# A hand-written order of units, whole-tile splits and step-free turns in the feed-forward nets of a two-layer fp32 block

## The chip, the cores and the metric

The kernel runs on one core of one Trainium2 chip. The metric is device time in microseconds (us) of the whole program, the median of several runs. Profiles are one traced execution each; times inside a trace count from the first instruction.

## The reference, cut to what matters

One sequence of 256 tokens of width 1024 goes through two layers. Each layer is a feed-forward net (FFN), a token mixer, a cross attention to 256 memory rows, and a second FFN, each followed by a layer norm:

```python
for l in range(DEPTH):                                   # DEPTH = 2
    h = layer_norm(ALPHA * h + 0.5 * swiglu(h, ffn1_gate[l], ffn1_up[l], ffn1_down[l]), ...)
    z = h @ w_in[l]                                      # mixer: short conv, linear recurrence, pooling
    ...
    h = layer_norm(ALPHA * h + mix @ w_out[l], ...)
    h = layer_norm(ALPHA * h + cross_attn(h, mem, ca_q[l], ca_k[l], ca_v[l], ca_o[l]), ...)
    h = layer_norm(ALPHA * h + 0.5 * swiglu(h, ffn2_gate[l], ffn2_up[l], ffn2_down[l]), ...)

def swiglu(x, w_gate, w_up, w_down):                     # 1024 -> 2816 -> 1024
    return (silu(x @ w_gate) * (x @ w_up)) @ w_down
```

## The kernel before, in words

**Precision.** Every fp32 operand of a product is split into a high part (`hi`, rounded by a copy on ScalarE, ACT) and the rest (`lo`, a subtraction on VectorE, DVE). `split` (L60 to L62) is this pair: L61 on ACT, then L62 on DVE, which reads what L61 wrote. A product is three matmuls (`mm_rows`, L130): hi*hi, hi*lo, lo*hi. L106 is the line of nearly every matmul.

**Weights.** `load` (L64) brings weights from device memory in pieces of 1 MB (a `raw` tile of 128 x 2048, three of them in a ring, fetched on the SyncE queue, SP) and splits each piece in two halves of 128 x 1024 into `whi` and `wlo` tiles, eight of each. A half's tiles come free when its last matmul is done.

**FFN.** 2816 hidden columns go in five chunks of 512 and one of 256. Of a chunk there are two pieces of the gate weights, two of the up weights and two of the down weights. `hidden` (L488) computes gate and up for both halves of the tokens (i = 0, 1), `activate` and `gated` (L405, L408) evict them, `turn` (L415) brings the result to hidden-by-token form: four DMAs (`dealt<-sg`) and two 32x32-block transposes on DVE (L422), whose input and output both run in steps, then a split. Rows of the down weights are fetched strewn (`strewn`, L79: partition p takes rows 4p to 4p+3), which is the order that the stepped turn leaves. `both` (L556) adds a down piece into four PSUM tiles. Chunks are interleaved: gate and up of chunk c, then the second half of down of c-2, then the first half of c-1. The last three down pieces are the tail: `finish` (L292) runs them once for each of the four (token half i, column half n) and evicts each with the layer norm's steps L320 (residual), L322 (statistics), L324, L326, L327 (on GpSimd, POOL), L330 and L334.

**Token-major to width-major.** The next stage needs the normed `h` transposed (`xT`). For token half 0 this is done by eight TensorE (PE) transposes (L170, `transposed`) inside the last part of the tail. For token half 1 the function that `finish` returns, `pend`, is called by the next stage between its products; the first chunk of an FFN (`first`, L428) computes i = 0 of gate, half of up, then calls `pend`, then goes on. After `ffn1`, whose follower is the mixer, token half 0 takes another way: `deal` (L532) copies `h` on ACT in steps, sends it through four DMAs, and `dealt` transposes it on DVE (L546) and splits it with stepped writes after the norm of half 1. Keys of the attention (`keys`, L599) run between `ffn1` and the mixer, and there `pend` stands before the fourth of four column products.

**Order.** The instruction order of each engine is made by a scheduler from priorities (order of the program text) and modelled times; it puts another ready instruction between two that depend on each other. `tc.manual_schedule(engines=...)` keeps the instructions of a block in their written order on the engines named, while instructions from outside the block may still come between. Before the change only the start of the first FFN (PE, ACT, DVE), the mixer (PE) and the recurrence's end (DVE) are written by hand.

Of the kernel before, what the change touches and what calls it, by code (L numbers as in the profile page):

```python
# [8 lines left out]
F32 = mybir.dt.float32  # L9
# [5 lines left out]
E = mybir.EngineType  # L15
# [16 lines left out]
PAD = 16  # L32


class Weights:
# [5 lines left out]
    def at(self, k, cols):  # L41
        j, kk = divmod(k, self.per)
        return self.hi[j][:, kk, cols], self.lo[j][:, kk, cols]


@with_exitstack
def model(ctx: ExitStack, tc: tile.TileContext, t: dict, out: bass.AP):
# [16 lines left out]
    def load(src, k0, nk, c0, ncol, fine=False, strewn=False):  # L64

        hi, lo, todo = [], [], []
        step = 2048 // ncol
        for a in range(k0, k0 + nk, step):  # L70
            raw = wp.tile([P, 2048], F32, tag="raw", name="raw", bufs=3)
            raw = raw.rearrange("p (k c) -> p k c", c=ncol)
            half = step // 2
            part = 1 if fine else step
            for b in range(0, step, part):
                loads.append(nc.sync.dma_start(
                    raw[:, b : b + part, :],
                    src[:, c0 : c0 + ncol].rearrange("(p k) c -> p k c", p=P)[:, a + b : a + b + part, :]
                    if strewn  # L79
                    else src[(a + b) * P : (a + b + part) * P, c0 : c0 + ncol].rearrange("(k p) c -> p k c", p=P),  # L80
                ))
            for s in range(2):
                h = wp.tile([P, 1024], F32R, tag="whi", name="whi", bufs=8)
                w = wp.tile([P, 1024], F32R, tag="wlo", name="wlo", bufs=8)
                h = h.rearrange("p (k c) -> p k c", c=ncol)
                w = w.rearrange("p (k c) -> p k c", c=ncol)
                r = raw[:, s * half : (s + 1) * half, :]
                if fine:
                    todo += [(h[:, b, :], w[:, b, :], r[:, b, :]) for b in range(half)]
                else:  # L90
                    split(h, w, r)
                hi.append(h)
                lo.append(w)
        return Weights(hi, lo, half, todo)
# [29 lines left out]
    def add(dst, o):  # L124
        dst = dst if len(dst.shape) == 3 else halves(dst)
# [27 lines left out]

    jdn = cst.tile([P, P], F32, name="jdn")
# [12 lines left out]
    def transposed_half(src, i, j, dh, dl, unit=idn):  # L167
# [3 lines left out]
        split(dh[:, 4 * j : 4 * j + 4, tok(i)], dl[:, 4 * j : 4 * j + 4, tok(i)], pt)  # L171

    def transposed(src, i, dh, dl, unit=idn):
        for j in range(2):
            transposed_half(src, i, j, dh, dl, unit)
# [28 lines left out]
    rows = cst.tile([P, P], F32, name="rows")  # L204
# [10 lines left out]
    def small_parameters(op):  # L215
        nc.gpsimd.memset(rows, 0.0)
# [68 lines left out]
    def ln_params(l, n):  # L285
        g = wp.tile([P, DM], F32, tag="lng", name="lng")
        b = wp.tile([P, DM], F32, tag="lnb", name="lnb")
        nc.sync.dma_start(g, t["ln_g"][l, n : n + 1, :].to_broadcast([P, DM]))
        nc.sync.dma_start(b, t["ln_b"][l, n : n + 1, :].to_broadcast([P, DM]))
        return g, b  # L290

    def finish(mm, y, scale, gb, last=False, flip=False, deal=None):  # L292
# [6 lines left out]
        for i in range(NT):  # L299
# [8 lines left out]
            for c in pieces:  # L308
# [37 lines left out]
    def project_back(slabs, late, gb, scale, between=lambda: None):  # L346
# [30 lines left out]
        return finish(tail, y, scale, gb)  # L377
# [681 lines left out]
```

## Time and profile before

| | |
|---|---|
| device time, 3 runs | 1097.89, 1098.06, 1099.81 us; median 1098.06 us |
| span of the profiled execution, first to last instruction | 1094.9 us; no device time is given for this execution by itself, the runs above lie 3.0 to 4.9 us over its span |
| granted PE clock | 0.998 |
| PE busy | 1079.6 us (99%), 6035 matmuls |
| DVE busy | 836.3 us (76%), of this 468.8 us in 388 `wlo` splits of 128x1024 |
| ACT busy | 585.0 us (53%), of this 398.0 us in 388 `whi` casts of 128x1024 |
| device memory read | 216.15 MB |

In the rows of the trace a line has the start, the time of the merged group, the engine, the source line, the operation, the tiles (written<-read), the shape and a count; what stands in brackets is idle time of that engine before it and what ended it.

### The profile page before, as it was taken

The numbers are of one execution on the slowest core, as the hardware profiler recorded it, in microseconds if no ns is written. First come the engines' busy times: TensorE is split into PE (matmuls) and PEld (weight loads), VectorE is DVE, ScalarE is ACT, GpSimd is POOL, SyncE is SP. The second block draws the span as 40 slices with busy tenths as digits, with TensorE's granted clock in tenths as the row PEclk, the third lists the DMA queues.
The fourth block names the chain that finished last, engine by engine and source line by source line (L and its number), as shares of the span: only waits on it lengthen the run. The fifth ranks groups of instructions, "written<-read, shape, count | busy, mean of one in ns | idle before, by whom it ended". The sixth has DMA issues, their size and how long they took to land.

```text
span 1094.9 us, 15563 instructions
## 1 busy us (share of the span) xinstructions
PE 1079.6 (99%) x6035; PEld 952.6 (87%) x6035; DVE 836.3 (76%) x1075; ACT 585.0 (53%) x811; POOL 61.0 (6%) x113
## 2 busy tenths in 40 slices
PE   9999999999999999999999999999999999999997
PEld 7888888889898888888888888888898988888886
DVE  6679678898889877666687655798988888766665
ACT  6456454767556455444455445457774644544450
POOL 9500001000000000000000000010000000000000
PEclk9999999999999999999999999999999999999999
DMA  9986665754575486766488666647536664876641
GB/s 326 302 285 226 212 215 170 244 180 164 185 273 176 141 293 217 237 214 217 154 266 265 218 216 206 231 143 261 183 135 217 229 208 163 259 242 211 219 167 38
DMA packets 123818, 232.90 MB, mean 213 GB/s; under 512 B 6432, under 2 KB 46656, under 8 KB 118624
## 3 DMA queue, kind: packets, MB, share of 16 engines
q1 hardware_dynamic: 121952, 229.53, 62.9%
q0 software_dynamic: 1216, 1.20, 0.4%
q8 instruction: 47, 0.77, 0.3%
q10 hardware_dynamic: 576, 1.18, 0.3%
q14 instruction: 27, 0.22, 0.1%
HBM read 216.15 MB, written 1.05 MB: 198 GB/s over the span
## 4 chain that ended last, share of the span: by engine, by line
PE 90%; DVE 7%; ACT 2%; issue 1%; DMA 0%; DVEq 0%; ACTq 0%
PE acc L106 60%; PE dn L106 27%; DVE wlo L62 2%; PE acc L170 1%; DVE square L971 1%; PE dn L766 1%; ACT xT L61 0%; DVE qTl L62 0%; DVE h L334 0%; ACT whi L61 0%; DMA h<-in_x_dram 0%; DVE h L330 0%; PE dn L825 0%; DVE xT L62 0%; DVE st L322 0%
## 5 line engine op out<-in xcount | busy, mean ns | idle before, releaser
L62 DVE TENSOR_TENSOR wlo<-raw,whi 128x1024 fp32r<-128x1024 f32 (+1 forms) x396 | 474.1, 1213 | 181.4 <-ACT whi L61 170.6
L61 ACT CAST whi<-raw 128x1024 fp32r<-128x1024 f32 (+1 forms) x396 | 402.5, 1040 | 312.4 <-PE dn L106 117.3
L106 PE MATMUL acc<-whi,xT 128*128 128x512 f32 x1312 | 395.0, 380 | 0.0
L106 PEld LDWEIGHTS acc<-whi,xT 128*128 128x128 f32 x1312 | 247.8, 189 | 35.2
L106 PE MATMUL acc<-wlo,xT 128*128 128x512 f32 x656 | 248.6, 379 | 0.0
L106 PE MATMUL acc<-xT,whi 128*128 128x512 f32 x576 | 142.6, 382 | 4.0 <-DVE xT L62 4.0
L106 PEld LDWEIGHTS acc<-wlo,xT 128*128 128x128 f32 x656 | 124.0, 189 | 17.5
L106 PE MATMUL dn<-whi,ah 128*128 128x512 f32 x346 | 131.3, 379 | 0.0
L106 PE MATMUL dn<-wlo,ah 128*128 128x512 f32 x346 | 131.1, 379 | 0.0
L106 PE MATMUL dn<-whi,al 128*128 128x512 f32 x346 | 131.1, 379 | 0.0
L106 PEld LDWEIGHTS acc<-xT,whi 128*128 128x128 f32 x576 | 103.8, 190 | 16.3 <-ACT whi L61 4.6
L106 PE MATMUL dn<-whi,xT 128*128 128x512 f32 x288 | 88.8, 383 | 0.0
L106 PEld LDWEIGHTS acc<-xT,wlo 128*128 128x128 f32 x576 | 75.6, 191 | 4.3 <-DVE wlo L62 0.4
L106 PE MATMUL acc<-xT,wlo 128*128 128x256 f32 x576 | 76.4, 275 | 0.0
L106 PEld LDWEIGHTS dn<-wlo,ah 128*128 128x128 f32 x346 | 65.4, 189 | 9.3
L106 PEld LDWEIGHTS dn<-whi,al 128*128 128x128 f32 x346 | 65.4, 189 | 9.3
L106 PEld LDWEIGHTS dn<-whi,ah 128*128 128x128 f32 x346 | 65.4, 189 | 9.2
L422 DVE STREAM_TRANSPOSE square<-dealt 128x512 f32<-128x512 f32 x40 | 63.8, 1658 | 0.8 <-DMA dealt<-sg 0.7
L327 POOL TENSOR_TENSOR rs<-rs,nhalf 128x1 f32<-128x1 f32 x16 | 14.9, 929 | 867.3 <-DVE rs L326 859.8
L106 PEld LDWEIGHTS dn<-whi,xT 128*128 128x128 f32 x288 | 54.4, 190 | 8.5 <-DVE xT L62 1.1
L106 PE MATMUL dn<-wlo,xT 128*128 128x512 f32 x144 | 54.7, 380 | 0.0
L320 DVE SCALAR_TENSOR_TENSOR h<-h,dn 128x512 f32<-128x512 f32 x31 | 21.2, 684 | 31.4 <-PE dn L106 31.4
(206 smaller groups left out, 980.3 us busy)
## 6 DMA issues: line engine op xcount, KB each, us to landing
raw<-in_ffn_up_dram SPq DMA_DIRECT2D x44, 1024.0 KB, 4.9
raw<-in_ffn_down_dram SPq DMA_DIRECT2D x44, 1024.0 KB, 5.1
raw<-in_ffn_gate_dram SPq DMA_DIRECT2D x42, 1024.0 KB, 5.0
raw<-in_w_in_dram SPq DMA_DIRECT2D x24, 1024.0 KB, 4.9
dealt<-sg SPq DMA_DIRECT2D x88, 128.0 KB, 3.2
raw<-in_ca_k_dram SPq DMA_DIRECT2D x8, 1024.0 KB, 5.0
raw<-in_w_out_dram SPq DMA_DIRECT2D x8, 1024.0 KB, 4.7
raw<-in_ca_v_dram SPq DMA_DIRECT2D x8, 1024.0 KB, 4.9
```

What stands on the lines that cost most here:

```text
L61: nc.scalar.copy(hi, src)
L62: lows.append(nc.vector.tensor_tensor(lo, src, hi.bitcast(F32), op=ALU.subtract))
L106: nc.tensor.matmul(o, w, x, start=start, stop=stop)
L170: nc.tensor.transpose(pt[:, k, :], src[:, (4 * j + k) * P : (4 * j + k + 1) * P], unit)
L320: nc.vector.scalar_tensor_tensor(v, v, ALPHA / scale, sums(y[i][n]), op0=ALU.mult, op1=ALU.add)
L327: nc.gpsimd.tensor_tensor(rs, rs, nhalf[:, 0:1], op=ALU.pow)
L422: nc.vector.transpose(d.rearrange("p k (i b) -> p b k i", b=4), x[:, :, i, :].rearrange("p b (j k) -> p b k j", k=4))
L766: nc.tensor.matmul(o[g, hh, :], kc[:, hh, g], x, start=True, stop=True)
L971: nc.vector.transpose(pt.rearrange("p m (i r b) -> p b (m i) r", i=2, b=4), pr[hh])
```

## The change

1. `split_tiles`: four `whi` and four `wlo` tiles of 128x2048 in place of eight of 128x1024. In the FFNs a piece is split by one ACT cast and one DVE subtraction of 128x2048. `load`, which serves the other stages and the first chunk of the program, still splits in halves, but both halves lie in one tile, which comes free as a whole.
2. The FFNs are lists of units of 12 matmuls (`plain_chunk`, `down_chunk`; `half_chunk` for the last 256 columns). `run_units` writes them, and `pump` queues, after the unit that uses a piece last, the split of the next piece; at the start it queues four. Everything in it is kept in this order on PE, DVE and ACT. The order of the products is the one of before, by four rows of k for each token half in place of two.
3. The turn: the deal's DMAs are queued at once, the transposes and splits two units later (`defer`). The transposes read and write without steps (`(b r)`, `(k j)`). For that the tokens of `xT` stand in another order inside an FFN (identity `pdn` with permuted columns in the transposes), and down rows are fetched in four DMAs of 32 partitions for each piece (`down_piece`). In the last, narrow chunk the evictions write in steps to undo the token order.
4. `deal` of the mixer's tokens is gone: after `ffn1` token half 0 is transposed on PE within the tail as elsewhere.
5. Smaller: `ah`, `al` have two buffers in place of three and `sg` two in place of one, except in the first FFN; `lng`, `lnb` are one tile `gb`; `rows` lies in another pool. `BLOCKS` is empty, so the functions for block products (`block_chunk`, `forms`, `blocked`) are there but produce no instruction.

The diff, cut to its core:

```diff
+    RAW = 3
+    WIDE = 4
+    def split_tiles(ncol):
+        h = wp.tile([P, 2048], F32R, tag="whi", name="whi", bufs=WIDE)
+        w = wp.tile([P, 2048], F32R, tag="wlo", name="wlo", bufs=WIDE)
 ...
     def load(src, k0, nk, c0, ncol, fine=False):
-            for s in range(2):
-                h = wp.tile([P, 1024], F32R, tag="whi", name="whi", bufs=8)
-                w = wp.tile([P, 1024], F32R, tag="wlo", name="wlo", bufs=8)
 ...
+            h, w = split_tiles(ncol)
+                for b in range(0, step, step // 2):
+                    split(*(x[:, b : b + step // 2, :] for x in (h, w, raw)))
 ...
+    pdn = cst.tile([P, P], F32, name="pdn")
+    nc.vector.tensor_copy(
+        pdn.rearrange("p (r b) -> p r b", b=4), idn.rearrange("p (b r) -> p r b", b=4)
+    )
 ...
-    def finish(mm, y, scale, gb, last=False, flip=False, deal=None):
+    def finish(mm, y, scale, gb, last=False, units=(idn, idn)):
-                        None if last or not i or not n or deal else lambda: transposed(h[0], 0, xTh, xTl),
+                        None if last or not i or not n else lambda: transposed(h[0], 0, xTh, xTl, units[0]),
-            if deal and not i:
-                dealt = deal(h[0])
-        if deal:
-            dealt()
-        return lambda: transposed(h[1], 1, xTh, xTl, jdn if flip else idn)
+        return lambda: transposed(h[1], 1, xTh, xTl, units[1])
 ...
+            def turn(c, x):
+                ah, al = act_tiles()
+                for i in range(NT):
+                    d = fp.tile([P, 4, P], F32, tag="up", name="square")
+                    nc.vector.transpose(
+                        d.rearrange("p k (b r) -> p b k r", b=4), x[:, :, i, :].rearrange("p b (k j) -> p b k j", j=32)
+                    )
+                    split(ah[:, :, tok(i)], al[:, :, tok(i)], d)
-                        d.rearrange("p k (i b) -> p b k i", b=4), x[:, :, i, :].rearrange("p b (j k) -> p b k j", k=4)
 ...
+                def prepare():                                  # of piece(...)
+                    p.hi, p.lo = split_tiles(p.ncol)
+                        split(p.hi, p.lo, p.raw)
 ...
+            def down_piece(c, u):
+                        src = down[c * CHUNK : (c + 1) * CHUNK].rearrange("(a k j) c -> a j k c", a=4, j=32)
+                        for a in range(4):
+                            loads.append(nc.sync.dma_start(
+                                raw[a * 32 : a * 32 + 32], src[a, :, 2 * u : 2 * u + 2, :]
+                            ))
 ...
+                        if a == 1 and kind == "gate":           # a unit of plain_chunk, after its 12 matmuls
+                            activate(state["s"], i, o)
+                        if a == 1 and kind == "up":
+                            gated(state["s"], i, o)
+                            if i == 1:
+                                x = deal(state["s"])
+                                defer(lambda: turn(c, x), 2)
 ...
+                            add(                                # half_chunk
+                                (s if kind == "gate" else r)[:, j, :].rearrange("p (i b r) -> p i r b", i=NT, b=4),
+                                mm_cols(w, slice(j * P, (j + 1) * P), xT).rearrange("p x h (r b) -> p x h r b", b=4),
+                            )
 ...
+                def pump(free):                                 # run_units
+                    live -= free
+                    while True:
+                        while fetched < len(order) and (raws < RAW if order[fetched].ring else order[fetched].free()):
+                            order[fetched].fetch()
+                            raws += order[fetched].ring
+                            fetched += 1
+                        if made == len(order) or live == WIDE:
+                            return
+                        order[made].prepare()
+                        raws -= order[made].ring
+                        live += 1
+                        made += 1
+
+                pump(0)
+                for x, (ws, run) in enumerate(units):
+                    for f in [f for at, f in waiting if at <= now[0]]:
+                        f()
+                    run()
+                    now[0] += 1
+                    pump(sum(final[w] == x for w in ws))
 ...
+                if pend is not None:                            # sequence
+                    seq += [g[0][0], g[1][0], u[0][0], call(pend), u[1][0], g[0][1], g[1][1], u[0][1], u[1][1]]
+                for c in range(1, end_chunk):
+                    for x in (*g, *u):
+                        seq += x
+                    if c > 1:
+                        seq += downs[c - 2][1]
+                    seq += downs[c - 1][0]
 ...
+            end = [down_piece(end_chunk - 1, 0), down_piece(end_chunk - 1, 1), down_piece(end_chunk, 0)]
+            with tc.manual_schedule(engines=ffn_engines):       # PE, DVE, ACT
+                run_units(sequence(), end)
```

More of the change, by code (lines that the diff above doesn't have):

```diff
@@ L584, in ffn @@
-            end = [slab(4, 0), slab(4, 1), slab(5, 0)]
-            def tail(i, m, cols, alone, between):
-                for u, a in enumerate(end):
-                    if between is not None and u == 1:
-                        between()
-                    for k in range(2):
-                        first = alone is not None and u == 0 and k == 0
-                        rows_of(a, i, k, m, first, u == 2 and k == 1, cols, alone)
-            mixer_next = name == "ffn1"
-            return finish(tail, ys, 0.5, gb, last=last, flip=mixer_next, deal=deal if mixer_next else None)
+                ah, al = act_rows(c, i, 2 * u + k)
@@ L599, in keys @@
+            return finish(tail, ys, 0.5, held["gb"], last=last, units=(idn, jdn) if name == "ffn1" else (pdn, pdn))
     def keys(l, c, between={}):
@@ L1030, in model @@
         pend = attention(l, pend)
[L1031 removed]
+        pend = ffn(l, "ffn2", 3, pend, last=l == DEPTH - 1, blocks=BLOCKS[2 * l + 1])
 _INS = [
```

549 lines of the change are left out of this document (368 added, 181 removed).

## The prediction

> **What bounds the kernel now.** I read the page's busy times first, then its slices, then stretches of the FFNs, then the few waits of TensorE (PE).
>
> ```profile
> span 1094.9 us, 15563 instructions
> PE 1079.6 (99%) x6035; PEld 952.6 (87%) x6035; DVE 836.3 (76%) x1075; ACT 585.0 (53%) x811; POOL 61.0 (6%) x113
> PE   9999999999999999999999999999999999999997
> ```
>
> PE is busy for all but 15.3 us. A busy PE can still be waiting a little between pipelined matmuls, so the spacing inside the FFNs decides (windows: time, then busy time and count for PE, PEld, DVE, ACT, POOL, clock, DMA share, GB/s; the sum is over 384 to 520, 557 to 690 and 925 to 1056).
>
> ```profile
> 384.00:520.00 136.00, 136.00 (x636) 119.20 (x635) 93.92 (x88) 67.79 (x77) 0.00 (x0) 1.00 0.72 235
> sum 400.00, PE 400.00 PEld 350.40 DVE 273.12 ACT 198.25 POOL 0.00; mean PE 133.33 PEld 116.80 DVE 91.04 ACT 66.08 POOL 0.00
> ```
>
> 636 matmuls in 136 us are 214 ns each, without a gap: a unit of 12 takes 2.57 us, a piece (24) 5.13 us. DVE has 127 us free of 400 there, ACT 202. So inside an FFN there is nothing to win: what DVE and ACT save there lies beside a full PE. The change computes the same products, so it can win or lose only where PE waits now, or where it will.
>
> **The change part by part.**
>
> **The deal after ffn1 goes.** Waits (count, longest), then the timeline of layer 0 and one set of eight transposes elsewhere:
>
> ```profile
> PE acc L106 <- DVE xT L62: 4.0, 2, 2.0
> ...
> 186.84 1.30 DVE L546 STREAM_TRANSPOSE square<-dealt 128x512 f32<-128x512 f32 x2
> 188.73 2.13 DVE L62 TENSOR_TENSOR xT<-square,xT 128x512 fp32r<-128x512 f32 x2 [0.29 <-ACT xT L61]
> 193.68 1.75 PE L106 MATMUL acc<-xT,whi 128*128 128x512 f32 x7 [2.02 <-DVE xT L62]
> ...
> 371.59 1.04 PE L170 MATMUL acc<-idn,h 128*128 128x128 f32 x8
> 372.38 0.46 PE L106 MATMUL dn<-whi,xT 128*128 128x512 f32 x1
> ```
>
> These two waits, 2.0 us in each layer, are where the mixer's first product waits for the second token half, whose split stood on DVE behind 3.4 us of the deal's transposes and stepped splits (1.30 + 2.13). They go, and with them two ACT copies, four DMAs on SP and the stepped casts. In their place the splits of token half 0 (1.28 us for a pair, quoted below) stand earlier, in the tail, and eight transposes on PE, which cost it 372.38 - 371.59 = 0.79 us. DVE is 2.1 us lighter before the wait, so I take the 2.02 as gone; what is late next is the `lo` half of w_in, needed 1.7 us later. Net 2.02 - 0.79 = 1.23 us won, twice: -2.5. Ends: -2.5 (wait gone whole) and +1.6 (wait stays, transposes added).
>
> **Wide splits where a stage begins with `pend`.** This happens three times: attention to ffn2 in both layers, ffn2 to ffn1 between them. The first, ACT, then DVE, then PE:
>
> ```profile
> 371.19 2.00 ACT L61 CAST whi<-raw 128x1024 fp32r<-128x1024 f32 x2 [12.02 <-PE dn L106]
> 373.10 1.05 ACT L61 CAST xT<-acc 128x512 fp32r<-128x512 f32 x2
> 374.05 3.88 ACT L61 CAST whi<-raw 128x1024 fp32r<-128x1024 f32 x4
> ...
> 372.35 2.34 DVE L62 TENSOR_TENSOR wlo<-raw,whi 128x1024 fp32r<-128x1024 f32 x2
> 374.61 1.28 DVE L62 TENSOR_TENSOR xT<-acc,xT 128x512 fp32r<-128x512 f32 x2
> 375.81 0.68 DVE L320 SCALAR_TENSOR_TENSOR h<-h,dn 128x512 f32<-128x512 f32 x1
> 376.40 1.22 DVE L62 TENSOR_TENSOR wlo<-raw,whi 128x1024 fp32r<-128x1024 f32 x1
> 377.54 0.69 DVE L322 BATCH_NORM_STATS2 st<-h 128x6 f32<-128x512 f32 x1
> 378.14 1.21 DVE L62 TENSOR_TENSOR wlo<-raw,whi 128x1024 fp32r<-128x1024 f32 x1
> 379.26 0.20 DVE L324 BATCH_NORM_AGGREGATE mv<-st 128x2 f32<-128x12 f32 x1
> 379.38 1.17 DVE L62 TENSOR_TENSOR wlo<-raw,whi 128x1024 fp32r<-128x1024 f32 x1
> 380.53 1.41 DVE L330 SCALAR_TENSOR_TENSOR h<-h,mv,lng 128x512 f32<-128x512 f32 x2
> 381.86 1.41 DVE L334 SCALAR_TENSOR_TENSOR h<-h,rs,lnb 128x512 f32<-128x512 f32 x2
> 383.18 1.22 DVE L62 TENSOR_TENSOR wlo<-raw,whi 128x1024 fp32r<-128x1024 f32 x1
> 384.31 1.29 DVE L62 TENSOR_TENSOR xT<-acc,xT 128x512 fp32r<-128x512 f32 x2
> ...
> 375.49 0.59 PE L106 MATMUL acc<-whi,xT 128*128 128x512 f32 x2
> 382.82 1.22 PE L170 MATMUL acc<-idn,h 128*128 128x128 f32 x8
> ```
>
> Here DVE has no gap from 372.35 to 385.6, and PE is fed with no slack: the `xT` subtraction of token half 0 has its first result near 375.3, the matmul that reads it starts at 375.49; the norm of half 1 ends at 383.27, while its eight transposes run on PE from 382.82. A microsecond more on DVE before the norm's end is a microsecond of PE. The change adds two things there.
>
> (a) The hand-over. Of the second gate piece the two casts ran 371.19 to 373.19 and the subtractions began at 372.35, after the first half. A whole-tile subtraction can begin only when the whole cast is done, at 373.19: 0.84 us that DVE idles, since nothing else is ready (the `xT` casts come after). A wide cast should be slightly shorter than two halves, so 0.8.
>
> (b) One more half ahead of the norm. The scheduler fills the pauses between L320, L322, L324 and L326 with ready splits: three halves of the up pieces stood there, the fourth after the norm, at 383.18. Whole tiles fill two pauses and take both up pieces, four halves, ahead: one half more, 384.31 - 383.18 = 1.13 us. What a wide subtraction saves is bounded by two groups of the list:
>
> ```profile
> L62 DVE TENSOR_TENSOR wlo<-raw,whi 128x1024 fp32r<-128x1024 f32 x388 | 468.8, 1223 | 181.4 <-ACT whi L61 170.6 <-PE acc L106 7.8
> L62 DVE TENSOR_TENSOR wlo<-raw,whi 128x512 fp32r<-128x512 f32 x8 | 5.3, 701 | 0.0
> ```
>
> By their slope 2048 columns take 1223 + 2 * 522 = 2.27 us, against 2.34 for a pair: 0.07 saved for a piece. So (b) is 1.0, and each place loses 1.8 us: +5.4 for three. The other two places have the same rows:
>
> ```profile
> 545.34 2.35 DVE L62 TENSOR_TENSOR wlo<-raw,whi 128x1024 fp32r<-128x1024 f32 x2
> 555.81 1.22 PE L170 MATMUL acc<-idn,h 128*128 128x128 f32 x8
> 912.40 2.34 DVE L62 TENSOR_TENSOR wlo<-raw,whi 128x1024 fp32r<-128x1024 f32 x2
> 922.88 1.22 PE L170 MATMUL acc<-idn,h 128*128 128x128 f32 x8
> ```
>
> From the subtraction to the transposes it is 10.47, 10.47 and 10.48 us. Ends of this term: 0 (the queue puts the up pieces behind the norm and the casts early) and +7 (2.3 each, a wide subtraction more ahead of the norm).
>
> **The first wide split, in the attention's tail.** The first gate piece is split while the last heads are evicted:
>
> ```profile
> 356.17 1.99 ACT L61 CAST whi<-raw 128x1024 fp32r<-128x1024 f32 x2
> 357.24 2.36 DVE L62 TENSOR_TENSOR wlo<-raw,whi 128x1024 fp32r<-128x1024 f32 x2 [0.26 <-ACT whi L61]
> 359.52 1.28 DVE L62 TENSOR_TENSOR xT<-acc,xT 128x512 fp32r<-128x512 f32 x2
> ```
>
> PE needs that `xT` at once (its tail units follow). The same hand-over moves it by 358.16 - 357.24 = 0.9; I take 0.8, in two layers: +1.6. Ends 0 and +4, if the cast also comes ahead of a head's eviction.
>
> **Covered, at nothing.** The step-free turn saves DVE about 1 us of 1.66, by the two kinds of transposes:
>
> ```profile
> L422 DVE STREAM_TRANSPOSE square<-dealt 128x512 f32<-128x512 f32 x40 | 63.8, 1658 | 0.8 <-DMA dealt<-sg 0.7
> dealt<-sg SPq DMA_DIRECT2D x88, 128.0 KB, 3.2
> raw<-in_ffn_down_dram SPq DMA_DIRECT2D x44, 1024.0 KB, 5.1
> ```
>
> 1658 ns against 0.65 for the mixer's step-free ones (186.84): 40 us of DVE, all inside FFNs beside a full PE. The new wait is the turn's: it stands in the DVE and ACT queues two units after its chunk's end, waits for deals that land about 6 us after that end (four issues, 3.2 to landing), and one split stands behind it. That split is then done near 13 us, and its piece is due four pieces on, at 20 us: 7 us of cover. In every other place four wide tiles give three pieces, 15 us, of lead over about 4.3 us for a cast and a subtraction. Two buffers of `ah` hold a turn until the unit after it is done (2.57 us), inside that cover. The narrow chunk's stepped evictions cost perhaps 0.3 us each (a stepped subtraction took 1.07 of 512 columns, above) ahead of two units of down. The down pieces' four issues for one put some 2 us for a chunk on SP, which is otherwise waiting. The copy that makes `pdn` ends before the first `h` lands. Coarser release in mixer and attention: up to a quarter piece (1.3 us) later for one split, in places where a whole load is ahead; 0, ends -1 and +2.
>
> **Sum.** -2.5 + 5.4 + 1.6 = +4.5 us on the profiled execution's span: 1099.4. The median of the runs, 1098.06, is 3.2 us over that span, for what lies around it, so 1102.6.
>
> **The rivals.**
>
> *Hand-over only (same).* The scheduler places the up pieces behind the norm, so (b) is nothing. For it: modelled times, not these, make the order. Against: the pauses were filled in all three places. 5 * 0.8 - 2.5 = +1.5: 1099.6.
>
> *The starts are covered (faster).* The one mechanism: in its fixed order DVE takes the small `xT` and norm steps first at the starts, the wide splits after, and the piece of PE work in hand (5.13 us) covers them. It decides from the point where less than 2.5 us is lost over all five places, 0.5 each. For it: over the whole of a start DVE has no more work than before. Against: zero slack at 375.49 and 382.82. -2.5: 1095.6, more if the mixer's own small gaps shrink.
>
> *The down pieces become a bound (slower still).* They now arrive in four parts of 32 partitions. The DMA share in FFNs is 0.72, a third of it down. If these took over 2.17 times as long, the sum would pass 1; at 2.25 times it is 0.72 * (2/3 + 0.75) = 1.02, 2% of 20 chunks of 30.8 us: +12, with the deal's gain 1108. For it: 128 KB into 32 partitions landed in 3.2 us, 1 MB into 128 in 5.1, five times slower a byte. Against: most of the 3.2 is latency and waiting behind other transfers. [...]
>
> **How the numbers follow.** Forecast 0.45, hand-over only 0.27, covered 0.16, transfers 0.12. A measurement of this kernel can tell about 0.2% (2.2 us) from no change. Faster 0.16, same 0.27, slower 0.57. The forecast's own range is 1100.3 to 1104.6; from 1095.4 to 1107 it takes in the covered case's middle and leaves out most of the transfers' one, about 2 in 10.
>
> **What would show it.** In the changed profile: PE without the 2.0 us wait before the mixer, and eight transposes in ffn1's tail; at the three starts the group of transposes later by near 1.8 us relative to the first gate matmul, with a PE wait on `xT` or `h`, and 128x2048 subtractions between L320 and L324; the tail of the attention later by 0.8 us. Transposes of L422's kind near 0.65 us and no other change of the time. Wrong would be: PE full at the starts, or PE waiting inside FFNs for `whi` with ACT waiting for `raw<-in_ffn_down_dram`.

## The result and the profile after

The changed kernel takes 1154.85 us (median of 4 runs, 1153.67 to 1157.82), the kernel before 1097.98: a ratio of 1.052, 95% interval 1.0501 to 1.0538. It is slower, as forecast, but by 57 us where 4.5 were worked out. From the page of the changed kernel, busy times and the 40 slices of PE and of its clock:

```profile
span 1154.1 us, 15394 instructions
PE 1097.6 (95%) x6051; PEld 958.5 (83%) x6051; DVE 787.6 (68%) x944; ACT 560.2 (49%) x679; POOL 62.1 (5%) x113
PE   9998998999999999999989999999999999999996
PEclk9999898999999999999989999999999999999999
```

The span grew by 59.2 us. PE stands idle for 1154.1 - 1097.6 = 56.5 us (15.3 before): 41.2 us more. It is busy 18.0 us longer, of which sixteen more transposes are under 2. Four stretches (from 114.5, 175.9, 203.2 and 582.1 us, 23.9 us together) have a granted clock of 0.50; PE is busy for 20.2 us in them, so about 10 of the rest are matmuls at half speed. The kernel before has no such stretch before its last matmul. The other 6 us are not explained. DVE and ACT have less work than before, so neither became a bound. Where the time goes, by stretches (columns as in the prediction):

```profile
384.00:520.00 136.00, 132.95 (x622) 115.48 (x621) 78.47 (x70) 52.56 (x42) 1.85 (x2) 1.00 0.70 201
...
115.00:125.00 10.00, 8.42 (x27) 6.69 (x28) 8.08 (x6) 7.87 (x6) 0.00 (x0) 0.69 0.55 173
```

The window of the FFN that held 636 matmuls in 136 us holds 622, and from 115 to 125 PE runs at a clock of 0.69. The groups of the list (the last numbers are the idle time before them and what ended it) say what PE waits for, and what its feeders wait for:

```profile
L123 PE MATMUL acc<-wlo,xT 128*128 128x512 f32 x656 | 250.3, 382 | 12.8 <-DVE wlo L75 12.8
L123 PE MATMUL dn<-wlo,ah 128*128 128x512 f32 x346 | 134.0, 387 | 10.1 <-DVE wlo L75 10.1
L123 PE MATMUL dn<-whi,ah 128*128 128x512 f32 x346 | 131.8, 386 | 6.2 <-ACT whi L74 6.2
L74 ACT CAST ah<-square 128x512 fp32r<-128x512 f32 x40 | 24.7, 619 | 225.0 <-DVE square L435 225.0
L435 DVE STREAM_TRANSPOSE square<-dealt 128x512 f32<-128x512 f32 x40 | 28.2, 707 | 131.4 <-DMA dealt<-sg 131.4
```

PE waits for weight splits: L123 are the matmuls, L74 a cast on ACT, L75 a subtraction on DVE, L435 the turn's transposes. The splits stand behind the turn: its transposes (0.71 us each, 0.65 predicted) hold DVE idle for 131.4 us until a deal lands, 20 times, and its casts hold ACT for 225 us. The deals land late (KB each, median us from issue to landing):

```profile
raw<-in_ffn_down_dram SPq DMA_DIRECT2D x160, 256.0 KB, 6.1
dealt<-sg SPq DMA_DIRECT2D x80, 128.0 KB, 7.2
```

7.2 us, where it was 3.2. One such place in the timeline, DVE, ACT, SP and PE (L420 is the gated product that ends a chunk, L428 issues the deals, L480 the down pieces):

```profile
505.15 1.28 DVE L420 TENSOR_TENSOR sg<-acc,sg 128x512 f32<-128x512 f32 x2
506.35 2.28 DVE L75 TENSOR_TENSOR wlo<-raw,whi 128x2048 fp32r<-128x2048 f32 x1
517.23 0.71 DVE L435 STREAM_TRANSPOSE square<-dealt 128x512 f32<-128x512 f32 x1 [8.60 <-DMA dealt<-sg]
522.48 6.70 DVE L75 TENSOR_TENSOR wlo<-raw,whi 128x2048 fp32r<-128x2048 f32 x3 [1.10 <-ACT whi L74]
...
518.03 0.62 ACT L74 CAST ah<-square 128x512 fp32r<-128x512 f32 x1 [12.59 <-DVE square L435]
520.55 5.49 ACT L74 CAST whi<-raw 128x2048 fp32r<-128x2048 f32 x3
...
506.46 2.68 SPq L428 DMA_DIRECT2D dealt<-sg  x4
509.26 17.26 SPq L480 DMA_DIRECT2D raw<-in_ffn_down_dram  x8
...
522.50 0.48 PE L123 MATMUL acc<-whi,xT 128*128 128x512 f32 x1 [0.40 <-ACT whi L74]
524.83 0.48 PE L123 MATMUL acc<-wlo,xT 128*128 128x512 f32 x1 [1.84 <-DVE wlo L75]
```

The chunk's last eviction ends at 506.43. Until the transposes start at 517.23, DVE does one subtraction; two pieces that landed at 508.0 and 514.4 stand unsplit behind the turn, with a third that lands at 519.95, and all three come in a bunch from 520.55. PE has worked off what was split at 522.10, 15.7 us after the eviction, and stops. Behind fourteen of the twenty turns PE stops in this way within 14 us, for 0.55 to 3.90 us, 25 us in all; behind the other six it does not.

### The profile page after: what moved, and what is told of

Its sections match the earlier page's. It is cut to its first block, busy times and chain, and to the rows that moved or that the text cites. A ratio compares the mean times of both kernels' runs of the same rounds, so it can differ in the third digit from the quotient of the medians.

```text
span 1154.1 us, 15394 instructions
## 1 busy us (share of the span) xinstructions
PE 1097.6 (95%) x6051; PEld 958.5 (83%) x6051; DVE 787.6 (68%) x944; ACT 560.2 (49%) x679; POOL 62.1 (5%) x113
## 5 line engine op out<-in xcount | busy, mean ns | idle before, releaser
L75 DVE TENSOR_TENSOR wlo<-raw,whi 128x2048 fp32r<-128x2048 f32 (+2 forms) x268 | 454.4, 1716 | 144.8 <-ACT whi L74 138.4
L74 ACT CAST whi<-raw 128x2048 fp32r<-128x2048 f32 (+2 forms) x268 | 379.2, 1444 | 198.8 <-PE dn L123 56.6
L123 PE MATMUL acc<-whi,xT 128*128 128x512 f32 x1312 | 397.9, 381 | 3.3 <-DVE xT L75 2.1
L123 PEld LDWEIGHTS acc<-whi,xT 128*128 128x128 f32 x1312 | 248.7, 190 | 41.4 <-DVE xT L75 3.2
L123 PE MATMUL acc<-wlo,xT 128*128 128x512 f32 x656 | 250.3, 382 | 12.8 <-DVE wlo L75 12.8
L123 PEld LDWEIGHTS acc<-wlo,xT 128*128 128x128 f32 x656 | 124.6, 190 | 33.1 <-DVE wlo L75 15.9
L123 PE MATMUL dn<-wlo,ah 128*128 128x512 f32 x346 | 134.0, 387 | 10.1 <-DVE wlo L75 10.1
L123 PE MATMUL acc<-xT,whi 128*128 128x512 f32 x576 | 142.6, 383 | 0.3 <-DVE xT L75 0.3
L123 PE MATMUL dn<-whi,ah 128*128 128x512 f32 x346 | 131.8, 386 | 6.2 <-ACT whi L74 6.2
L74 ACT CAST ah<-square 128x512 fp32r<-128x512 f32 x40 | 24.7, 619 | 225.0 <-DVE square L435 225.0
L123 PE MATMUL dn<-whi,al 128*128 128x512 f32 x346 | 133.0, 384 | 0.0
L435 DVE STREAM_TRANSPOSE square<-dealt 128x512 f32<-128x512 f32 x40 | 28.2, 707 | 131.4 <-DMA dealt<-sg 131.4
L123 PEld LDWEIGHTS acc<-xT,whi 128*128 128x128 f32 x576 | 103.8, 190 | 12.8 <-DVE xT L75 1.1
L123 PE MATMUL dn<-whi,xT 128*128 128x512 f32 x288 | 88.6, 382 | 0.3
L123 PEld LDWEIGHTS dn<-wlo,ah 128*128 128x128 f32 x346 | 66.6, 192 | 21.9 <-DVE wlo L75 12.3
L123 PEld LDWEIGHTS dn<-whi,ah 128*128 128x128 f32 x346 | 66.5, 192 | 17.1 <-ACT whi L74 7.4
L123 PEld LDWEIGHTS acc<-xT,wlo 128*128 128x128 f32 x576 | 75.6, 191 | 4.6 <-DVE wlo L75 0.7
L123 PE MATMUL acc<-xT,wlo 128*128 128x256 f32 x576 | 76.4, 275 | 0.1
L123 PEld LDWEIGHTS dn<-whi,al 128*128 128x128 f32 x346 | 66.6, 192 | 9.5
L123 PEld LDWEIGHTS dn<-whi,xT 128*128 128x128 f32 x288 | 54.2, 189 | 8.9 <-DVE xT L75 1.1
L123 PE MATMUL dn<-wlo,xT 128*128 128x512 f32 x144 | 54.8, 380 | 0.2 <-DVE wlo L75 0.2
```

The costliest lines, as they stand in the source:

```text
L74: nc.scalar.copy(hi, src)
L75: lows.append(nc.vector.tensor_tensor(lo, src, hi.bitcast(F32), op=ALU.subtract))
L123: nc.tensor.matmul(o, w, x, start=start, stop=stop)
L435: nc.vector.transpose(d.rearrange("p k (b r) -> p b k r", b=4), x[:, :, i, :].rearrange("p b (k j) -> p b k j", j=32))
```

## The experiments

Ratios are to the kernel before, which was at 1097.87 to 1097.98 in every comparison. Line numbers are those of the kernel that a row is from; in the changed kernel and its variants L192 is a transpose on PE, L355 the last step of the norm and L416 the activation of the gate, beside those named above. "Hand order" is the fixed list of PE, DVE and ACT, "scheduler's order" the fixed list of PE alone.

| DVE's and ACT's list | down piece in four 32-partition transfers | in one of 128 |
|---|---|---|
| hand order, turn two units behind its deal | 1154.85 (the change) | 1145.58 |
| hand order, turn six units behind | 1130.88 | |
| hand order, six, last full chunk two | 1117.9 | 1109.56 |
| scheduler's order | 1169.87 | 1108.27 |

**One transfer for a down piece**, in the changed kernel (the turn then reads in steps again):

```diff
-  for a in range(4):
-      loads.append(nc.sync.dma_start(raw[a * 32 : a * 32 + 32], src[a, :, 2 * u : 2 * u + 2, :]))
+  loads.append(nc.sync.dma_start(raw, src[:, 2 * u : 2 * u + 2, :]))     # rows "(p k) c -> p k c"
```

> The changed kernel with one edit: a down piece is again one transfer into 128 partitions (partition p takes rows 4p to 4p+3), and the turn reads its input in steps to fit it, as before; it still writes without steps. Theory A (the four transfers of 32 partitions are slow, 4 KB packets near 300 ns for 159, and through the deals behind them hold the turn that stands at the head of the fixed DVE and ACT queues): 1099 to 1104 us, the deals land in 3 to 4 us again, ACT waits for the turn under 60 us for 225. Rival B (the fixed order of DVE and ACT is what costs, whatever the transfers do): above 1135. Rival C (both a half): near 1125.

1145.58 us (1144.38 to 1147.14), ratio 1.0431 (1.0417 to 1.0445): 9 of the 57 us, rival B. The waits (in total, count, longest) show the turn as it was, and the deals still land late:

```profile
ACT ah L74 <- DVE square L435: 226.9, 40, 12.1
DVE square L435 <- DMA dealt<-sg: 107.3, 20, 8.2
...
dealt<-sg SPq DMA_DIRECT2D x80, 128.0 KB, 6.7
```

The narrow transfers alone are not the cause while the turn stands early, and they are not what makes the deals late. They land when the weight pieces ahead of them have landed: the last piece issued before a turn's deals lands 6.8 us (median) after the first of the deals is issued in the changed kernel and 6.7 here, the deals themselves in 7.2 and 6.7. In the kernel before it is 1.3, and the deals land in 3.2. (The stepped transposes take 1.5 us in place of 0.71 here, which is against this run.)

**A later turn**, in the changed kernel:

```diff
-  defer(lambda: turn(c, x), 2)
+  defer(lambda: turn(c, x), 6)
```

> The changed kernel with the turn queued six units after its chunk in place of two, so 15 us later in place of 5; the four transfers of a down piece stay. Theory A with its amplifier (slow transfers cost only because the turn waits for the deal in front of the next splits): most comes back, 1102 to 1115 us, and DVE waits for the deals under 20 us for 131. If the slow transfers starve the casts directly (raw late): above 1135, with ACT's waits for raw at 100 us or more. Rival B without the turn (the order of the splits alone): above 1135 with casts that wait for PE.

1130.88 us (1128.85 to 1133.67), ratio 1.0298 (1.0281 to 1.0315). That is between the ranges that were expected. The middles of the FFNs are whole again: 629 matmuls from 384 to 520, and PE is idle there for 1.0 us, at a start. What is left sits at the ends of the FFNs, for instance (PE):

```profile
558.76 1.75 PE L192 MATMUL acc<-pdn,h 128*128 128x128 f32 x8 [3.21 <-DVE h L355]
563.32 1.22 PE L123 MATMUL acc<-whi,xT 128*128 128x512 f32 x2 [1.96 <-DVE xT L75]
```

Six units after the last full chunk the block is nearly over, and the order of the tail's products comes out otherwise: the four residual steps (L341), each behind the products of one column half, start within 3.6 us here (552.35 to 555.93), in the next kernel over 9 us (548.15 to 557.20). The next kernel has the first of the two stops as well (3.31 us), but 0.36 in place of the second and a clock of 1.00, where here it is 0.50 for 10.2 us from 559.2. So:

**The turn moved, but not the last one**: `defer(lambda: turn(c, x), 2 if c == end_chunk - 1 else 6)`. TensorE's list is that of the changed kernel.

> The changed kernel with one number altered: the turn of a chunk is queued six units behind its deal in place of two, but the turn of the last full chunk of each block stays at two. TensorE's list is then exactly that of the changed kernel, and only the places of the turn's steps in VectorE's and ScalarE's lists differ. Theory A (the turn stands at the head of two queues before its deal has landed, and the weight splits wait behind it): 1105 to 1113 us, that is the kernel before, less 4.6 for the deal into the mixer, plus 5 to 7 for the starts, plus the stall of the one early turn that is left in each of four blocks, 2 to 3 each; the middles of the blocks show no stop of TensorE. Rival T (the transfers themselves are too slow): above 1125. Rival E (the rest of the late-turn kernel's loss was not the order of the tails): no better than that kernel, 1128 to 1134.

1117.9 us (1113.4 to 1119.22), ratio 1.0176 (1.0152 to 1.02): 37 of the 57 us by moving steps in two queues, nothing else changed; 5 us more are left than theory A's range ended at. Waits, and the stretch of the FFN:

```profile
ACT ah L74 <- DVE square L435: 103.0, 38, 10.8
DVE square L435 <- DMA dealt<-sg: 26.5, 5, 7.6
```

```profile
384.00:520.00 136.00, 135.00 (x630) 118.02 (x629) 80.02 (x60) 58.39 (x45) 0.92 (x1) 1.00 0.85 230
```

Only the five turns that were not moved (four block ends and the first chunk's) still have DVE wait for a deal. With the four narrow transfers in place and PE nearly full, the DMA share is 0.85.

**This and one transfer.**

> The kernel above (turn at six, last full chunk at two) with each piece of the down matrix in one transfer of all 128 partitions. Theory A: with the turns out of the way a slow transfer is hidden in the middles and only shortens the stall of the early turn at the block ends, so 0 to 4 us below the kernel above, 1102 to 1112. Rival T: the transfers are half of what is left, 8 or more below it.

1109.56 us (1108.79 to 1110.87), ratio 1.0109 (1.0094 to 1.0124): 8 us less. Theory A had 0 to 4 and the rival 8 or more, so the transfers' own price was set too low. Together with the two runs above this makes a square: the later turn gives 37 us with narrow transfers and 36 with full ones, the full transfer 9 with the early turn and 8 with the late one. By the spacing of matmul starts the ends of the first three FFNs lose 2 to 3 us less each, and the program's last steps end 2.5 us sooner behind the last matmul. The two profiled executions differ by 3.8 us only (1113.4, the fastest of its four, and 1109.65), so some 4 of the 8 us are in no trace.

**This, one transfer and half splits at the starts**: the four pieces of the first chunk with `half=True` where `pend` is open.

> The kernel above (turn moved, one fetch) with the four pieces of the first chunk of a block split in two halves each where the block begins with a norm that is still open (three blocks). The prediction's starts term: 5 to 7 us below the kernel above (1.8 predicted and about 2.4 read from the trace at each of three starts). Rival: the loss at the starts is not the width of the split, 0 to 1 below it.

1108.8 us (1102.46 to 1110.19), ratio 1.0081 (1.0049 to 1.0114). At the starts it does what was expected (by the spacing of matmul starts 6.2 us over the three; shown below with a kernel where nothing hides it), but in the profiled run a new stop at an early turn, 2.92 us up to 718.5, and the slow matmuls behind it (48 in 13.68 us, 0.285 each for 0.214) take it back. The total, with its wide spread, decides nothing.

**All turns moved**, with one transfer and the half splits: the last to four units, the very first chunk's from none to six.

> The kernel with the turn moved, one fetch and half splits at the starts, with two more turns moved: that of the last full chunk of each block to four units behind its deal (two before), and that of the very first chunk, which stood directly behind its deal, to six units. Theory A: the stops of TensorE that the former kernel's trace still shows around these five turns (4.8 us at 100 to 125, 3.6 at 150 to 175, 6.2 at 700 to 725, by the excess of matmul starts over their steady spacing) go, which gives 1093 to 1099 us, no slower than the kernel before. Rival E (a later last turn makes the tails late, as in the late-turn kernel): 1107 to 1120.

1110.29 us (1106.41 to 1114.22), ratio 1.0110 (1.0079 to 1.0141): no gain. That lies in the rival's range, but the tails of the other three FFNs are not the cause. The stop at 700 went, that at 150 to 175 too; the one at 100 to 125 stayed, since it is not the turn's alone (below); two new ones came in the first FFN, one of 3.87 us up to 55.5 and one of 4.3 in two parts (2.85 and 1.41) at its end. This FFN shares the DMA engines with the memory rows (32 transfers of 32 KB, 6.3 us to landing) and has one `sg` buffer. ACT at the first:

```profile
46.04 1.09 ACT L416 ACTIVATE sg<-acc 128x512 f32<-128x512 f32 x2 [5.36 <-DMA dealt<-sg]
...
54.80 0.62 ACT L74 CAST ah<-square 128x512 fp32r<-128x512 f32 x1 [3.35 <-DVE square L435]
```

The next chunk's activation waits until the deal has read the one buffer, and PE stops 3.87 us for the turn's cast at 54.80 (its down product reads `ah`). A place that is right for one block is wrong in another.

**The scheduler's order**, in the changed kernel: `ffn_engines = {E.PE}`.

> The changed kernel with the hand-made order on TensorE alone: VectorE's and ScalarE's lists are left to the scheduler, which puts the turn's casts behind the gate activations of the next chunk. Splits stay wide, the down pieces stay four transfers. Theory A: the loss in the middles goes, 1105 to 1130 (the tails' order is the scheduler's too, so the loss at the block ends may be as in the late-turn kernel). Rival T: the transfers cost the time whatever the order, 1140 to 1155. A third way: the scheduler's own order also puts a step that waits for a transfer ahead of weight splits, 1130 to 1200, and then the trace shows which.

1169.87 us (1167.07 to 1172.36), ratio 1.0656 (1.0631 to 1.0681): the third way. DVE in one chunk, then the sum over the program (waits: total, count, longest):

```profile
493.40 0.69 DVE L420 TENSOR_TENSOR sg<-acc,sg 128x512 f32<-128x512 f32 x1 [5.72 <-PE acc L123]
496.06 0.69 DVE L420 TENSOR_TENSOR sg<-acc,sg 128x512 f32<-128x512 f32 x1 [1.97 <-PE acc L123]
496.66 4.48 DVE L75 TENSOR_TENSOR wlo<-raw,whi 128x2048 fp32r<-128x2048 f32 x2
```

```profile
DVE sg L420 <- PE acc L123: 102.1, 35, 7.9
```

It is the same fault with another step: here the gated products, which wait for PE, stand at the head of DVE's list for 7.7 us, ahead of a subtraction whose cast was done at 489.5; PE then stops 2.8 us for that `wlo`, up to 499.0. So a fixed list by hand is not needed for the fault.

**The scheduler's order and one transfer.**

> The kernel with the scheduler's own order on VectorE and ScalarE, with each piece of the down matrix in one transfer. If the four 32-partition transfers are what misleads the scheduler's order (it lets gated products, which wait for TensorE, stand ahead of the down pieces' splits), the loss goes: 1098 to 1112. If the order is bad whatever the transfer, or the wide split alone makes it so, it stays above 1140.

1108.27 us (1107.94 to 1109.36), ratio 1.0093 (1.0076 to 1.011): 62 us less by the shape of one transfer (and the turn's read steps that go with it), where it was 8 to 9 in the hand orders. The gated products no longer stand ahead of splits that are due; the same wait is now

```profile
DVE sg L420 <- PE acc L123: 7.9, 16, 1.3
```

Of what is left, about 6.6 us lie in the first 25 us by the spacing of matmul starts, where the hand-made order of the very first chunk went too.

**The kernel before with narrow transfers**: each strewn down piece in four transfers of 32 partitions.

> The kernel before with one edit: each strewn down piece comes in four transfers of 32 partitions, 8 KB runs as before. The order stays the scheduler's. Theory A: packets take about twice as long and a piece lands late, but nothing of a fixed order waits for it: 1098 to 1106 us. If the slow transfers alone make the loss: above 1130. If four transfers of 32 partitions are as fast as one: 1098 with packet times unchanged, and theory A falls.

1222.33 us (1220.23 to 1224.08), ratio 1.1128 (1.1112 to 1.1144), where theory A had 1098 to 1106. The order fails here as well, on SP (its waits; L424 issues the deals, L415 is the gated product):

```profile
SPq L424 <- DVE sg L415: 242.8, 20, 18.7
```

The deals, which wait for the gated products, stand ahead of parts of down pieces in SP's queue, 12 us each time, and PE waits for the casts of the pieces, up to 10.8 us. The deals land in 3.1 us here, since mostly no piece is in flight when they are issued. The run does not part the transfers' price from the queue's.

**Deals on POOL's queue**, in the changed kernel: `nc.gpsimd.dma_start` in `deal`.

> The changed kernel with the deals issued on POOL's queue in place of SP's; turns early, four transfers, order by hand as in the changed kernel. Theory A with its cause (the deals land late because they stand behind weight fetches that were issued on the same queue just before): the deals land in 3 to 4.5 us again in place of 7.2 and most of the stops go, 1105 to 1130. Rival: the DMA engines themselves are full at that place, whichever queue issues: landing stays at 6 us or more and the time at 1145 to 1165.

1194.54 us (1186.29 to 1203.04), ratio 1.0878 (1.082 to 1.0935): outside both ranges. Landing was no shorter:

```profile
dealt<-sg POOLq DMA_DIRECT2D x80, 128.0 KB, 7.7
```

So it is not the place in SP's queue alone that makes a deal late: the last weight piece issued before the deals lands 6.7 us (median) after the first of them here too, and from 510 to 514 in the changed kernel's trace the DMA engines are full (a share of 1.16, in the window shown below). The 7.7 us lie in the rival's range of 6 or more. The run changes more than the place, though: the trace has these deals as software_dynamic packets (11.69 MB in that queue, 1.20 in the changed kernel). The time rose by 40 us more; DVE waits 170.5 us for the deals in place of 131.4, which is as much, but why they come later still is open.

**What is left of the change**: the scheduler's order and one transfer, the first chunk's order by hand again, half splits at the three starts.

> The kernel with the scheduler's own order on VectorE and ScalarE and one transfer for a down piece (1108), with two more edits: the order of the very first chunk is kept by hand on all three engines as in the changed kernel, and the four pieces of the first chunk of a block are split in halves where a norm is still open. Theory A's sum: the first matmuls wait 6.6 us less at the start of the program, and the three starts give 1.85 each (1.23 and 1.13 before, 0.51 behind): 1094 to 1098 us. If the loss that is left were spread over the wide splits in the middles: above 1102.

1103.96 us (1103.67 to 1104.47), ratio 1.0056 (1.0039 to 1.0073). That is above 1102, as the rival had it, but not from the rival's cause: behind the first 25 us the spacing shows 11.7 us lost, against 10.7 in the kernel without the deal. The starts cost next to nothing; the program's start got worse, not better. PE at the first of the three starts, then DVE in the first chunk:

```profile
391.33 1.29 PE L192 MATMUL acc<-pdn,h 128*128 128x128 f32 x8 [0.35 <-DVE h L355]
...
16.02 0.37 DVE L284 TENSOR_SCALAR cnt<-cnt,wcol 128x16 f32<-128x16 f32 x2 [7.03 <-POOL cnt L274]
```

A small step that waits 7 us for POOL stands ahead of the subtractions, and PE stops 5.8 us for `xT`: once more a waiting step at the head of a list. By the spacing of matmul starts the first 25 us lose 13.8 us against 3.5 in the kernel without the deal (below). Without those 10.3 it would be 1093.7, an estimate, which is the time of that kernel (1093.25).

**The same with four transfers of all 128 partitions** (512 columns each).

> The kernel above with each down piece in four transfers again, but each over all 128 partitions (512 columns, 2 KB runs) in place of 32. If the number of transfers is what costs: above 1115. If it is that each goes to 32 partitions only: within 4 us of the kernel above.

1103.51 us (1103.23 to 1103.69), ratio 1.0052 (1.0037 to 1.0067): the same. It is the width in partitions that costs, not the number of transfers; runs of 2 KB, shorter than the 4 KB of the narrow transfers, cost nothing either. A quarter lands in 3.9 us here and in 6.1 in the changed kernel:

```profile
raw<-in_ffn_down_dram SPq DMA_DIRECT2D x160, 256.0 KB, 3.9
```

**The kernel before without the mixer's deal**: `deal=None` in the FFN's call of `finish`.

> The kernel before with one edit: after ffn1 the token half 0 is transposed on PE in the tail, the mixer's deal is gone. By the prediction's first term the 2.0 us wait before the mixer goes and 0.8 us of transposes come, in two layers: 1095.5 us (-2.5). Rival: the wait stays, as DVE is still behind with the weights of the mixer: 1098 to 1099.6.

1093.25 us (1093.19 to 1094.45), ratio 0.9956 (0.9943 to 0.997). This is the one version that beats the kernel before, by 0.4%. PE runs into the mixer's product without a wait:

```profile
191.74 0.38 PE L106 MATMUL acc<-mT,whi 128*128 128x512 f32 x1
191.95 1.67 PE L106 MATMUL acc<-xT,whi 128*128 128x512 f32 x7
```

## Why the prediction was right or wrong

**The mixer's deal: right, a little small.** -2.5 was worked out; the part alone gives -4.6 by the medians and 1094.9 - 1091.5 = -3.4 by the spans.

**The starts: right in mechanism and near in size.** 1.8 us each was predicted, by a hand-over of 0.8 and a half more of 1.0. The changed kernel, DVE, then PE:

```profile
396.67 2.29 DVE L75 TENSOR_TENSOR wlo<-raw,whi 128x2048 fp32r<-128x2048 f32 x1 [1.33 <-ACT whi L74]
400.67 2.29 DVE L75 TENSOR_TENSOR wlo<-raw,whi 128x2048 fp32r<-128x2048 f32 x1
403.48 2.28 DVE L75 TENSOR_TENSOR wlo<-raw,whi 128x2048 fp32r<-128x2048 f32 x1
...
399.62 0.70 PE L123 MATMUL acc<-whi,xT 128*128 128x512 f32 x2 [1.06 <-DVE xT L75]
408.19 1.29 PE L192 MATMUL acc<-pdn,h 128*128 128x128 f32 x8 [0.96 <-DVE h L355]
```

DVE idles for the whole-tile cast, two wide subtractions stand among the norm's steps, and PE stops for 1.06 and 0.96 us. With half splits 0.35 is left. The 6.2 us that half splits give back over the three starts are 2.1 each.

**The attention's tail: wrong, small.** +0.8 in each layer was expected. In the first layer the changed kernel's PE stops there for 0.59 and 0.07 us, all for DVE, and the kernel before for 0.52 and 0.35, for ACT and DVE: nothing is lost.

**"Covered, at nothing" is the step that failed.** It put the turn's deals at 6 us after the chunk's end with the 3.2 us landing of the trace of before, the split behind the turn at 13, its due time at 20, "four pieces on": 7 us of cover. Each of the three was off at the place shown. The deals landed 8.5 to 8.8 us after their issue instead of 3.2, at 515 to 517, because the change itself alters what shares the DMA engines with them: two up pieces, 2 MB, are issued at 503.04 and 505.26, just ahead. And the cover was three pieces, as the same passage says for "every other place": PE came to the piece after 15.7 us. With 5.5 us more of landing the split is done at 13 + 5.5 = 18.5; it was done at 18.4, and PE stopped for 0.40 and 1.84. Three splits came to stand behind the turn, not one; but PE stops for the first of them, so that alone cost nothing here. All twenty turns make DVE wait, fourteen make PE stop. That this wait is the cause, and not only beside it, the moved turn shows: 1154.85 to 1117.9. The row that should have been doubted was the 3.2: it was measured under other traffic. The prediction's sign of being wrong, PE waiting inside FFNs for `whi`, came, but ACT waited for the turn (225.0 us) and little for the down pieces (37.7).

**Some stops were paid twice.** No price was set on the clock. In the kernel with moved turns and one transfer, DVE, PE and two windows of 6 us:

```profile
100.76 0.69 DVE L75 TENSOR_TENSOR mT<-turned,mT 128x512 fp32r<-128x512 f32 x1 [0.68 <-ACT mT L74]
...
108.29 0.48 PE L123 MATMUL dn<-whi,ah 128*128 128x512 f32 x1 [0.94 <-ACT whi L74]
110.62 0.79 PE L123 MATMUL dn<-wlo,ah 128*128 128x512 f32 x1 [1.84 <-DVE wlo L75]
111.21 0.63 PE L123 MATMUL dn<-whi,al 128*128 128x512 f32 x1
111.63 0.63 PE L123 MATMUL dn<-whi,ah 128*128 128x512 f32 x1
```

```profile
110.50:116.50 6.00, 5.88 (x14) 4.71 (x15) 4.11 (x3) 4.74 (x4) 0.00 (x0) 0.50 0.62 192
116.50:122.50 6.00, 6.00 (x30) 5.26 (x29) 4.72 (x5) 2.78 (x2) 0.00 (x0) 1.00 1.03 371
```

After 2.8 us of stops the clock is 0.50 for 6 us: 14 matmuls where 28 fit at 0.214 us each, some 3 us more lost. This stop is not an early turn's. It is a like fault with a third kind of step: four pairs of a cast and a subtraction for the memory rows (`mT`), the last of them in the first row, take ACT and DVE from 93.4 to 101.5, each waiting for the other, and the turn's and the weight splits stand behind them. The changed kernel has it at 115.0 and 117.4 (3.53 and 1.53 us), every kernel in hand order near there, and the scheduler's order with one transfer does not.

**The rival "the down pieces become a bound" had 0.12 and 1108.** As a bound it did not come: with PE nearly full the share is 0.85 (with the turn moved, but not the last one), not 1. No row of before has a fetch of down rows into 32 partitions, so the 2.25 times behind the 1108 was the author's assumption. The trace of the changed kernel shows the direction, weight fetches over 128 partitions first, then a stretch of deals and narrow ones (472 and 320 KB by their packets, beside 144 KB of a full one):

```profile
505.00:507.00 2.00, 2.00 (x11) 1.76 (x10) 2.00 (x4) 0.44 (x1) 0.00 (x0) 1.00 1.01 388
510.00:514.00 4.00, 4.00 (x21) 3.49 (x20) 0.00 (x0) 0.00 (x0) 0.00 (x0) 1.00 1.16 240
```

240 GB/s in place of 388 with the DMA engines full (shares of 1.16 and 1.01): 0.62, for the mixed stretch. Single packets of 4 KB part them better: 159 ns (median) in the kernel before, where none is of a narrow fetch, and 313 from 88 to 97 us in the changed kernel, where they are of narrow down pieces, 1.97 times as long; the bound needed 2.17. What the prediction lacked was the way from there to the time: narrow pieces cost 8 us where PE's feeders are queued well, and 62 through the order that the scheduler then makes. The range ended at 1107 because each stall was priced where its own step stands; a step that waits in an in-order list delays all that stand behind it (at 517.23 a wait of 8.60 us, with two landed pieces behind it).

**The sum.** Without the 6.6 us of the program's start, the scheduler's order with one transfer would stand at 1101.7. That is near the 1102.6 of the prediction, and what this put at nothing (early turns, narrow transfers, the fixed order) is worth the other 53. The nearness is in part luck: that kernel is not the change, and by its parts the sum would be -4.6 for the deal, +6.2 for the starts and nothing for the attention's tail, +1.6 in place of +4.5; some 2 us more are not located.

## What to carry to other kernels

In a queue that is worked off in order, as the lists of DVE, ACT and SP were in these traces, the question for every step is not how long it takes but how long it can wait at the head, and how many steps that others are due behind it: put a step that waits for a transfer as late as its consumer allows, and count the cover to the first consumer behind it. A landing time read from a trace holds for the traffic of that trace (3.2 us before, 7.2 after); where a change alters the transfers beside it, price the landing again from the bytes that go ahead of it. An order, by hand or by a scheduler, is made for certain durations: change the shape of one transfer and look again at what stands in front of what on DVE, ACT and SP.

## What the runs showed of the hardware

- Four transfers of a megabyte piece land in 3.9 us each over 128 partitions (the last kernel with four transfers) and in 6.1 over 32 (the changed kernel); their number costs nothing that can be measured (1103.51 against 1103.96).
- The deals, four copies of 128 KB within the chip, land about when the weight pieces issued before them have landed, but by the median in no trace in less than 3.1 us. Where the last such piece lands 1.3, 4.1, 6.7 and 6.8 us after the first deal's issue (medians over the turns of the kernel before, the scheduler's order with one transfer, the changed kernel with one transfer, the changed kernel), the deals land in 3.2, 4.8, 6.7 and 7.2, whether the pieces are narrow or full.
- After two stops of 0.94 and 1.84 us with a single matmul between them, in the kernel with moved turns and one transfer, the granted clock was 0.50 for 6 us, and a matmul of 512 columns started every 0.43 us; matmuls were at full pace again 5.8 us after the last stop. In the changed kernel it was 0.50 for 6.83 us from 114.46, 175.90 and 582.09, beside stops of 3.53 us (up to 115.05), of 2.06 and 1.84 (up to 174.63 and 176.95) and of 3.44 (up to 582.51), and for 3.41 us from 203.21 behind one of 2.24 (up to 202.81). One of 2.44 up to 771.29 in the same trace had no such stretch, nor had one of 2.02 in the kernel before. So the length of a stop alone does not tell it here.
- The 32x32-block transpose of 512 columns takes 0.71 us with neither side in steps, and 1.55 with its input alone in steps:

```profile
L435 DVE STREAM_TRANSPOSE square<-dealt 128x512 f32<-128x512 f32 x40 | 61.9, 1549 | 13.8 <-DMA dealt<-sg 13.8
```

This is the kernel with moved turns and one transfer; the kernel before, with both sides in steps, had 1658 ns. So a stepped input has nearly the whole price; a stepped output alone was not run.
